# A decoder trunk on one core: the tile scheduler plans with its detailed timeline instead of a plain duration per instruction

## The chip, the cores and the metric

The kernel runs on one core of one Trainium2 chip. The time is device time in microseconds (us) of one execution, as the median of three runs of the kernel before: 2271.49 us (2265.71 to 2271.65). A core has five engines that each work through a list of instructions of their own, in order: PE (matmuls, with a weight load PEld for each), DVE (VectorE), ACT (ScalarE), POOL (GpSimd) and SP (SyncE, which here issues the DMAs). They wait for each other through semaphores.

## What is computed

Two residual layers and a final RMSNorm on an input of 1024 positions by 1024 channels, all float32. The even layer feeds dilated attention and a gated linear recurrence (HGRN2) from one projection; the odd layer is a gated DeltaNet with 16 value heads that share 8 key heads.

```python
def reference(x, norm_w, final_norm_w, even_w_in, even_w_out, hgrn_lb_logits, hgrn_norm_w,
              odd_w_in, odd_conv_w, odd_dt_bias, odd_a_log, odd_norm_w, odd_w_out):
    ...
    h = x
    for layer in range(DEPTH):
        hn = rms_norm(h, norm_w[layer])
        j = layer // 2
        if layer % 2 == 0:
            h = h + even_mixer(hn, even_w_in[j], even_w_out[j], lb_all[j], hgrn_norm_w[j])
        else:
            h = h + odd_mixer(hn, odd_w_in[j], odd_conv_w[j], odd_dt_bias[j], odd_a_log[j],
                              odd_norm_w[j], odd_w_out[j])
    return rms_norm(h, final_norm_w)
```

The part of the odd layer that matters here is the chunked delta rule. `sol` inverts a unit lower triangular matrix for each chunk, and `step` runs over the chunks in sequence, since each needs the state of the last:

```python
    lower = jnp.where(strict, jnp.einsum('bhnid,bhnjd->bhnij', kb, kc) * decay, 0.0)
    a_mat = lower + jnp.eye(C_CHUNK, dtype=jnp.float32)
    sol = lax.linalg.triangular_solve(a_mat, rhs, left_side=True, lower=True, unit_diagonal=True)
    ...
    def step(state, inp):
        u_n, w_n, a_n, qd_n, kt_n, gl_n = inp
        v_new = u_n - jnp.einsum('bhcd,bhdv->bhcv', w_n, state)
        o = jnp.einsum('bhcd,bhdv->bhcv', qd_n, state) + jnp.einsum('bhij,bhjv->bhiv', a_n, v_new)
        new_state = state * gl_n[..., None, None] + jnp.einsum('bhcd,bhcv->bhdv', kt_n, v_new)
        return new_state, o
```

## The kernel before

**Stages.** The kernel runs the norm and the transposes first (to about 57 us), then the HGRN2 heads of the even layer mixed with the projections of the next head (to about 460), the dilated attention with its output projection (to about 1060), the second norm and the odd layer's gates (to about 1210), the odd layer's eight heads (to about 2105), and its output projection with the final norm.

**Projections.** Every projection splits both operands into a high and a low part and accumulates three matmuls for each product (`mm3`, lines 151 to 153). In the rows of this document a matmul of these lines with the tile `pk`, `pv`, `pq` (the odd layer's key, value and query) or `oz` (its gate) is such a projection matmul of 128 by 512. They are called fill below: apart from their weights, they depend on nothing that the recurrence makes.

**A head of the odd layer** consists of four generators. `recur(hh)` (line 1149) goes through eight chunks of 128 positions. In chunk c, `vp` (L1197, PE) gives `vt` (L1200, DVE) and `vn` (L1202, ACT); `kv` (L1206, PE) takes `vt`, `op` (L1217, PE) takes `vn` and the attention tile `A` (L1170, DVE, from `qk`, L1168, PE); `kv` gives the new state `S` (L1210, DVE); the next chunk's `ks` (L1182, PE) and `qs` (L1188, PE) need `S`; `r` (L1185, DVE) comes from `ks`, `oq` (L1191, ACT) from `qs`, and the next `vp` needs `r`. `vp`, `qs` and `qk` share one PSUM bank (tag "d"), so that `vp` also has to wait until `oq` has read `qs`. `oj` (L1225, ACT) sums the squares of the output.

`invert(hh + 1)` (line 1044) prepares the triangular inverse of the next head. It has eight decay tables `gcl`, one for each chunk, which go through two buffers: a DMA (L1040), three activations on ACT (L1054 twice, L1055) and two operations on DVE (L1069), which scale `kk` (L1063, PE) into `L` and so set the buffer free. A 31-step substitution on DVE follows (L1084 and L1086), and then small matmuls. The recurrence has decay tables of its own (`gca`: DMA, POOL L1156, ACT L1158).

`proj(hh + 1)` (line 971) makes the next head's keys, values and queries, and first calls `way_out(hh - 1)` (line 1017) for the head before: `normed` (POOL L1005), the gate projection `oz` with its tile `g` (ACT L991, DVE L992, one buffer), the transposes `ot` (L1012, PE), `oy` (ACT L1013, POOL L1014) and a store to `ymix` (L1015).

**What sets the order.** The program is first written out in one sequence by generators that are mixed by weights:

```python
        for hh in range(8):
            fill = proj(hh + 1) if hh < 7 else seq(way_out(6), gate7(), out_last(range(3), ["pj"]))
            if hh < 7:
                fill = blend(invert(hh + 1), fill, 0.8)
            mix(recur(hh), fill, 2.8)
            drain(fill)
```

The tile scheduler of the context then sets each engine's order. It walks the program with that sequence as priority and, for each engine, issues in its planned time what is ready; the engines execute the resulting lists. Where `tc.manual_schedule` stands (PE in the attention, PE and DVE in its last part and the first output projection, lines 789 and 795) an engine keeps the order in which the program is written. Everything else on every engine goes by the planned time, which the scheduler before takes from a plain duration for each instruction. The context is opened in `kernel()`, below with the line numbers of the profile.

## Time and profile before

| | us |
|---|---|
| median of three runs | 2271.49 |
| lowest and highest | 2265.71, 2271.65 |
| the profiled execution | 2270.35 |
| its span, first to last instruction | 2268.6 |
| PE busy, share of the span | 2162.0, 95% |
| DVE busy | 1409.7, 62% |
| ACT busy | 950.0, 42% |
| POOL busy | 239.5, 11% |
| mean granted TensorE clock (1 is full speed) | 0.992 |

The profile's page gives the busy time of each engine, the span in 40 slices of equal length (a digit is the busy share in tenths; the row PEclk is the granted clock), and the costliest groups of instructions. The trace behind it answers by windows, by waits and by single rows in order of time. In a row of the timeline the first two numbers are the start and the duration in us; `[1.12 <-ACT oq L1191]` says that the engine sat idle for 1.12 us before it and that `oq` on ACT ended this.

### The profile page before, as it was taken

How to read it: one execution, taken by the hardware profiler on the slowest of the kernel's cores; microseconds unless marked ns; L12 is line 12 of the kernel's file. 1: busy time of each engine (PE TensorE's matmuls, PEld its weight loads, DVE VectorE, ACT ScalarE, POOL GpSimd, SP SyncE). 2: the span in 40 equal slices, each digit the busy share in tenths (PEclk: the TensorE clock that was granted, in tenths of full speed). 3: DMA queues.
4: the chain of work that ended last, by engine and by line, in shares of the span. 5: the costliest groups of instructions: out<-in, count | busy, mean ns of one | idle time of the engine just before them, and what ended most of it. 6: DMA issues, size and time to landing. Idle time of an engine off the chain costs nothing. (4 is left out here: it accounts for less than half of the span.)

```text
span 2268.6 us, 52553 instructions
## 1 busy us (share of the span) xinstructions
PE 2162.0 (95%) x21781; PEld 1760.6 (78%) x21781; DVE 1409.7 (62%) x3236; ACT 950.0 (42%) x2551; POOL 239.5 (11%) x252
## 2 busy tenths in 40 slices
PE   7999999999999999989999988989898999899998
PEld 6888888898877878767886776767777777678787
DVE  6353535453444344457776986968878787755767
ACT  5233333333232232222237664655555555544223
POOL 0010101010000000000000013121212121210000
PEclk9999999999999999989999999999999999999999
DMA  4111111114342334353233222121212122124233
GB/s 146 38 48 48 43 49 47 48 34 126 91 128 71 109 91 122 97 162 108 93 116 104 61 55 67 51 78 41 77 51 76 49 71 65 58 64 153 85 112 112
DMA packets 100079, 184.15 MB, mean 81 GB/s; under 512 B 12672, under 2 KB 30208, under 8 KB 99840
## 3 DMA queue, kind: packets, MB, share of 16 engines
q1 hardware_dynamic: 99840, 180.79, 25.9%
q8 instruction: 171, 2.80, 0.5%
q14 instruction: 68, 0.56, 0.1%
HBM read 151.25 MB, written 29.49 MB: 80 GB/s over the span
## 5 line engine op out<-in xcount | busy, mean ns | idle before, releaser
L117 DVE TENSOR_TENSOR w_lo<-raww,w_hi 128x512 fp32r<-128x512 f32 x292 | 210.2, 722 | 199.5 <-ACT w_hi L116 196.8
L116 ACT CAST w_hi<-raww 128x512 fp32r<-128x512 f32 x292 | 181.1, 620 | 298.0 <-DMA raww<-in_ewo_dram 51.0
L647 ACT ACTIVATE P<-P,nm 128x256 f32<-128x256 f32 (+7 forms) x128 | 71.4, 559 | 133.9 <-DVE nm L645 133.9
L151 PE MATMUL op<-w_hi,yplo 128*128 128x512 f32 x288 | 113.7, 395 | 3.3 <-DVE hr L296 1.7
L153 PE MATMUL op<-w_hi,yplo 128*128 128x512 f32 x288 | 112.2, 390 | 0.0
L152 PE MATMUL op<-w_lo,yplo 128*128 128x512 f32 x288 | 112.2, 390 | 0.0
L151 PE MATMUL oz<-hn_hi,w_hi 128*128 128x512 f32 x256 | 109.9, 429 | 0.0
L151 PE MATMUL pv<-hn_hi,w_hi 128*128 128x512 f32 x256 | 106.7, 417 | 0.5 <-ACT uv L899 0.5
L296 DVE TENSOR_TENSOR hr<-hr,op 128x512 f32<-128x512 f32 x128 | 85.9, 684 | 34.2 <-PE op L153 33.6
L153 PE MATMUL pv<-hn_hi,w_lo 128*128 128x512 f32 x256 | 104.1, 407 | 0.0
L152 PE MATMUL oz<-hn_lo,w_hi 128*128 128x512 f32 x256 | 103.0, 402 | 0.0
L153 PE MATMUL oz<-hn_hi,w_lo 128*128 128x512 f32 x256 | 102.5, 400 | 0.0
L152 PE MATMUL pv<-hn_lo,w_hi 128*128 128x512 f32 x256 | 102.2, 399 | 0.0
L653 DVE STREAM_TRANSPOSE PB<-P 128x256 f32<-128x256 f32 (+3 forms) x64 | 54.6, 853 | 72.8 <-ACT P L647 72.8
L1156 POOL TENSOR_TENSOR gca<-gca,MA 128x256 f32<-128x256 f32 x64 | 50.6, 791 | 453.8 <-DMA gca<-gcd 252.8
L296 DVE TENSOR_TENSOR hres<-hres,op 128x512 f32<-128x512 f32 x96 | 64.7, 682 | 31.8 <-PE op L153 29.4
L642 DVE CUSTOM_DVE_ANT_0 P<-S,G 128x256 f32<-128x256 f32 (+7 forms) x128 | 58.2, 492 | 36.8 <-PE S L638 35.2
L904 DVE SCALAR_TENSOR_TENSOR vT<-uv,cws,vT 128x512 f32<-128x512 f32 x96 | 74.3, 774 | 4.7 <-ACT vT L902 3.8
L1084 DVE TENSOR_TENSOR tm<-Lp,Tp 128x126 f32<-128x126 f32 (+22 forms) x248 | 74.9, 302 | 3.7
L1158 ACT ACTIVATE gca<-gca,g_ngc 128x128 f32<-128x128 f32 x128 | 45.8, 401 | 69.3 <-POOL gca L1156 69.1
L151 PE MATMUL avp<-w_hi,hn_hi 128*128 128x256 f32 x256 | 74.5, 291 | 0.0
L151 PE MATMUL op<-w_hi,yphi 128*128 128x512 f32 x160 | 65.9, 412 | 8.5 <-ACT yphi L116 4.6
(367 smaller groups left out, 6292.1 us busy)
## 6 DMA issues: line engine op xcount, KB each, us to landing
raww<-in_ew_dram SPq DMA_DIRECT2D x128, 256.0 KB, 3.0
raww<-in_ow_dram SPq DMA_DIRECT2D x100, 256.0 KB, 3.0
V<-vd SPq DMA_DIRECT2D x64, 256.0 KB, 5.3
rawy<-ymix SPq DMA_DIRECT2D x64, 256.0 KB, 2.7
raww<-in_ewo_dram SPq DMA_DIRECT2D x32, 256.0 KB, 3.0
gcl<-gcd SPq DMA_DIRECT2D x64, 128.0 KB, 3.0
gca<-gcd SPq DMA_DIRECT2D x64, 128.0 KB, 3.0
ymix<-oy SPq DMA_DIRECT2D x32, 256.0 KB, 2.0
```

The lines of the kernel that those rows point to most:

```text
L116: act.copy(hi, raw)
L117: dve.tensor_tensor(lo, raw, hi.bitcast(F32), op=ALU.subtract)
L151: pe.matmul(ps, lh, rh, start=start, stop=False)
L152: pe.matmul(ps, lh, rl, start=False, stop=False)
L153: pe.matmul(ps, ll, rh, start=False, stop=stop)
L296: dve.tensor_tensor(dst[:, n], src[:, n], ps, op=ALU.add)
L642: dve.tensor_tensor_reduce(Pm[:, e, w0:], S[e][:, w0:WG], G[:, w0:], 1.0, -3e38, op0=ALU.add, op1=ALU.max, accum_out=mx[:, e:e + 1])
L647: act.activation(Pm[:, e, w0:], Pm[:, e, w0:], AF.Exp, bias=nmx[:, e:e + 1], scale=0.125, accum_out=den[:, i, e:e + 1])
L653: dve.transpose(PB[:, :, i * WG + w0:(i + 1) * WG], Pm[:, :, w0:])
L904: dve.scalar_tensor_tensor(a[0][:, s], ub[:, i + s.start:i + s.stop], cws[:, tile_no, i:i + 1], a[0][:, s], op0=ALU.mult, op1=ALU.add)
L1084: dve.tensor_tensor(tm[:, :31 - k, :n], Lp[:, k, k + 1:, None].to_broadcast([P, 31 - k, n]), Tp[:, k:k + 1, :n].to_broadcast([P, 31 - k, n ...
L1156: pool.tensor_tensor(DA, DA, MA[:, None, :].to_broadcast([P, 2, 128]), op=ALU.add)
```

## The change

One argument of the tile context:

```diff
-    with tile.TileContext(nc) as tc:
+    with tile.TileContext(nc, schedule_with_timeline_sim=True) as tc:
         trunk_kernel(tc, *args)
```

The scheduler takes the planned time, which decides what is issued next on each engine, from its detailed timeline (a model of engines, semaphores and DMAs) instead of a plain duration for each instruction. No code of the kernel changes, and both kernels have the same instructions but for two loads of activation tables on ACT (26 before, 24 now). The order on all engines in the HGRN stage and in the odd layer is another; in the attention (some 500 to 1200 us) and from the last output projection on it stands as it was.

In the rows of order that follow, the digit after a tile's letters is the head, the next the chunk (`vp4_1` is `vp` of head 4, chunk 1), and the last number only tells tiles apart; "x2" stands for two instructions alike. `w46` and `w55` are weights, `hn` is the normed input, and `L4` holds head 4's inverse.

PE, before, from the end of head 3's recurrence into head 4's; the rows left out at "..." are projection matmuls of `oz` (11, 5 and 6 of them):

```order
L1168 MATMUL qk4_0_19968<-q4_19824,kT4_18183 128x128
L151 MATMUL oz3_0_0_19950<-hn_hi1_13909,w55_hi1_19639 128x512
...
L1012 MATMUL ot3_0_0_19988<-ident_69,bv3_18473 128x128 x4
L1197 MATMUL vp4_0_19996<-bv4_19691,L4_18651 128x128 x2
L151 MATMUL oz3_0_1_20003<-hn_hi0_13908,w55_hi0_19633 128x512
...
L1063 MATMUL kk5_1_20010<-kT5_19401 128x128 x4
...
L1206 MATMUL kv4_0_20044<-vt4_0_19999,kn4_18333 128x256
L1217 MATMUL op4_0_20048<-vn4_0_20001,A4_0_19970 128x128 x2
L1168 MATMUL qk4_1_20056<-q4_19824,kT4_18183 128x128
```

PE, of the change, at the same place, without a gap:

```order
L1197 MATMUL vp3_7_19780<-r3_7_19750,L3_17433 128x128 x2
L1063 MATMUL kk5_0_19876<-kT5_19401 128x128
L1217 MATMUL op3_7_19797<-vn3_7_19783,A3_7_19729 128x128 x2
L1168 MATMUL qk4_0_19968<-q4_19824,kT4_18183 128x128
L1197 MATMUL vp4_0_19996<-bv4_19691,L4_18651 128x128 x2
L1206 MATMUL kv4_0_20044<-vt4_0_19999,kn4_18333 128x256
L1217 MATMUL op4_0_20048<-vn4_0_20001,A4_0_19970 128x128 x2
L1168 MATMUL qk4_1_20056<-q4_19824,kT4_18183 128x128
L1182 MATMUL ks4_1_20089<-S4_0_20046,kT4_18183 128x256
L1063 MATMUL kk5_1_20010<-kT5_19401 128x128 x4
L1188 MATMUL qs4_1_20094<-S4_0_20046,q4_19824 128x256
L1197 MATMUL vp4_1_20112<-r4_1_20091,L4_18651 128x128 x2
```

No projection matmul stands between `vp` of chunk 7 and `vp` of chunk 2 of the next head; the fill that stood there now stands in the chunks before and after.

ACT, before, at `vn` of head 4's chunk 0 (`raww` is a weight being split):

```order
L1055 ACTIVATE gcl5_3_19895<-gcl5_3_19895 128x256
L1013 ACTIVATE oy3_0_0_19987<-ot3_0_0_19988,onws_14228 128x512
L1158 ACTIVATE gca4_2_20051<-gca4_2_20051,g_ngc_14219 128x128 x2
L1054 ACTIVATE gcl5_4_19902<-gcl5_4_19902,g_ngc_14219 128x128 x2
L1202 COPY vn4_0_20001<-vp4_0_19996 128x256
L1055 ACTIVATE gcl5_4_19902<-gcl5_4_19902 128x256
L1054 ACTIVATE gcl5_5_20015<-gcl5_5_20015,g_ngc_14219 128x128
L116 CAST w56_hi3_19944<-raww56_3_19946 128x512
```

ACT, of the change, from `vn` of head 3's last chunk to `vn` of head 4's chunk 0 and on:

```order
L1202 COPY vn3_7_19783<-vp3_7_19780 128x256
L1225 ACTIVATE oj3_7_0_19801,oss3_18645<-bv3_18473 128x128
L1225 ACTIVATE oj3_7_1_19803,oss3_18645<-bv3_18473 128x128
L1054 ACTIVATE gcl5_2_19888<-gcl5_2_19888,g_ngc_14219 128x128 x2
L1054 ACTIVATE gcl5_3_19895<-gcl5_3_19895,g_ngc_14219 128x128 x2
L1055 ACTIVATE gcl5_2_19888<-gcl5_2_19888 128x256
L1202 COPY vn4_0_20001<-vp4_0_19996 128x256
L1055 ACTIVATE gcl5_3_19895<-gcl5_3_19895 128x256
L1158 ACTIVATE gca4_2_20051<-gca4_2_20051,g_ngc_14219 128x128 x2
```

`vn` of chunk 0 came behind the activations of `gcl` 4; now it comes behind those of `gcl` 2 and 3, so that `gcl` 4 to 7 fall between the next chunks' `vn` and `oq`.

PE, before, in head 0 from `op` of chunk 3 to `vp` of chunk 4:

```order
L1217 MATMUL op0_3_15912<-vn0_3_15883,A0_3_15800 128x128 x2
L1168 MATMUL qk0_4_15920<-q0_15141,kT0_14333 128x128
L1182 MATMUL ks0_4_15935<-S0_3_15909,kT0_14333 128x256
L151 MATMUL oz0_0_0_16296<-hn_hi0_13908,w46_hi0_15818 128x512
L1188 MATMUL qs0_4_15940<-S0_3_15909,q0_15141 128x256
L152 MATMUL oz0_0_0_16296<-hn_lo0_13910,w46_hi0_15818 128x512
...
L1197 MATMUL vp0_4_15986<-r0_4_15937,L0_14534 128x128 x2
```

PE, of the change, in head 0 from `op` of chunk 3 to `op` of chunk 4, without a gap:

```order
L1217 MATMUL op0_3_15912<-vn0_3_15883,A0_3_15800 128x128 x2
L1168 MATMUL qk0_4_15920<-q0_15141,kT0_14333 128x128
L1182 MATMUL ks0_4_15935<-S0_3_15909,kT0_14333 128x256
L1188 MATMUL qs0_4_15940<-S0_3_15909,q0_15141 128x256
L1197 MATMUL vp0_4_15986<-r0_4_15937,L0_14534 128x128 x2
L1206 MATMUL kv0_4_16012<-vt0_4_15989,kn0_14523 128x256
L1217 MATMUL op0_4_16017<-vn0_4_15991,A0_4_15922 128x128 x2
```

In head 0 all eight chunks now stand on PE without a projection matmul; those that stood among them come ahead of its first `vp`.

## Prediction

> **What bounds the kernel now.** I read the page first, then the waits, then windows cut at the odd layer's heads, then the timeline inside them. The busy times, the 40 slices, and the longest waits of TensorE (engine, tile and line waited for, total us, times, longest):
>
> ```profile
> span 2268.6 us, 52553 instructions
> PE 2162.0 (95%) x21781; PEld 1760.6 (78%) x21781; DVE 1409.7 (62%) x3236; ACT 950.0 (42%) x2551; POOL 239.5 (11%) x252
> PE   7999999999999999989999988989898999899998
> DVE  6353535453444344457776986968878787755767
> ...
> PE op L1217 <- ACT vn L1202: 11.0, 14, 1.6
> PE nt L224 <- DVE xn L220: 10.5, 2, 8.3
> PE ks L1182 <- DVE S L1210: 9.7, 7, 1.8
> PE vp L1197 <- ACT oq L1191: 7.2, 10, 1.6
> ```
>
> PE bounds the kernel. Its amount of work does not change here, so the time is that work plus what PE loses in waits, and only the second part can move. Three of the four waits shown belong to `recur`, the delta-rule recurrence of the odd layer (`nt` is in the norms), and VectorE is close behind PE there (7 to 9 tenths). So I cut the odd layer where `vt` of chunk 0 starts in each head (columns: us, busy time of each engine, PEclk, DMA share, GB/s):
>
> ```profile
> 1319.00:1401.00 82.00, 71.26 (x543) 55.95 (x543) 63.59 (x177) 43.65 (x128) 20.06 (x24) 0.94 0.22 61
> 1401.00:1491.50 90.50, 84.73 (x619) 67.03 (x618) 74.94 (x219) 55.35 (x174) 18.69 (x21) 0.98 0.19 54
> 1491.50:1599.40 107.90, 98.21 (x697) 79.51 (x695) 85.25 (x232) 61.21 (x185) 20.84 (x23) 1.00 0.22 65
> 1599.40:1707.60 108.20, 99.93 (x698) 80.84 (x698) 85.51 (x226) 60.87 (x182) 20.88 (x23) 1.00 0.22 62
> 1707.60:1814.60 107.00, 99.72 (x698) 80.84 (x698) 85.11 (x226) 60.83 (x183) 22.12 (x25) 1.00 0.21 62
> ```
>
> "Busy" overstates PE, since pipelined matmuls overlap. The rhythm at which they follow each other is what one costs:
>
> ```profile
> 1505.43 0.60 PE L1206 MATMUL kv<-vt,kn 128*128 128x256 f32 x2
> 1505.87 0.61 PE L1217 MATMUL op<-vn,A 128*128 128x128 f32 x4
> 1506.31 0.39 PE L1168 MATMUL qk<-q,kT 128*128 128x128 f32 x2
> 1506.45 0.48 PE L151 MATMUL oz<-hn_hi,w_hi 128*128 128x512 f32 x1
> ...
> 1508.85 0.39 PE L152 MATMUL oz<-hn_lo,w_hi 128*128 128x512 f32 x1
> 1509.08 0.39 PE L153 MATMUL oz<-hn_hi,w_lo 128*128 128x512 f32 x1
> 1509.31 0.59 PE L1182 MATMUL ks<-S,kT 128*128 128x256 f32 x2
> ```
>
> A projection matmul costs 0.23 us (1508.85 to 1509.08), `kv` and `op` 0.44 each, `qk` 0.14. With `ks` and `qs` at about 0.43 and `vp` near 0.3 a chunk of the recurrence costs PE 2.0 us. A full head is 288 projection matmuls (66.3 us), eight chunks (16) and about 9 for inversion and transposes: 91 us of work in a window of some 108. **PE loses about 17 us per full head**, and by the same count 25 us in head 0 and 18 in head 1. Of some 155 us lost in eight heads, much could be gained or added to.
>
> **The change part by part.** No instruction of weight is added or removed (two activation-table loads on ACT go). The planner's order moves. The order of attention (500 to 1200 us) and of the tail stands as before: nothing to count. The HGRN stage and the odd layer are re-ordered.
>
> *Heads 3 to 5.* In the order before, the projection matmuls ahead of each `vp` of a head come 36, 30, 20, 22, 36, 42, 36 and 66 per chunk: spread. Afterwards 0, 0, 69, 66, 55, 55, 43 and 0. Thus from `vp` of chunk 7 to `vp` of chunk 2 of the next head PE has no fill: only 8.7 us of its own work (three chunks, `kk`, `ot`). This stretch also holds six of the eight rounds in which `invert` of the next head makes its decay tables (`gcl`, two buffers) and scales `kk`:
>
> ```profile
> 1403.21 1.13 DVE L1069 SCALAR_TENSOR_TENSOR L<-kk,sc,gcl 128x128 f32<-128x128 f32 x4 [0.49 <-PE kk L1063]
> ...
> 1420.55 0.60 DVE L1069 SCALAR_TENSOR_TENSOR L<-kk,sc,gcl 128x128 f32<-128x128 f32 x2
> ...
> L1054 ACT ACTIVATE gcl<-gcl,g_ngc x128: 384/392/433, 1235.7 to 1932.3; 128x128 f32<-128x128 f32 x128
> L1069 DVE SCALAR_TENSOR_TENSOR L<-kk,sc,gcl x128: 336/343/352, 1238.2 to 1933.9; 128x128 f32<-128x128 f32 x128
> L1040 SPq DMA_DIRECT2D gcl<-gcd x64: 319/320/1868, 1231.9 to 1928.2; - x64
> L1055 ACT ACTIVATE gcl<-gcl x64: 399/410/423, 1237.8 to 1933.2; 128x256 f32<-128x256 f32 x64
> ...
> DMA to landing us min/median/max: 2.8/3.0/5.2
> ```
>
> One buffer's round is a DMA of 3.0, ACT 2 x 0.39 + 0.41 and DVE 2 x 0.34: 4.9 us. After the first two, three rounds follow in each buffer: 14.7, with the first pair's 0.7 about 15.4 at least. The trace took 1403.2 to 1421.1, 17.9 us, in head 2's. ACT now holds `vn` and `oq`, for which PE's `op` and `vp` wait, in order behind `gcl` activations that wait for that DMA. So I set the stretch by the ring at 17.6 (nearest row 17.9, floor 15.4), plus a lead of 0.9 and some 3.3 until `vp` of chunk 2, whose ACT queue still holds `gca` (2 x 0.4), `oy`, `oj` and `g`: 21.8 us, 13 of them idle. SP and POOL do not relieve it: on SP the same `gcl` loads stand in the same sequence, only the `ymix` stores now come behind them; on POOL the multiplication at L1005 moves behind one more `gca`. The other 82 us of PE work then have 43 to 69 projection matmuls (10 to 16 us) per chunk beside the chain from one `vp` to the next:
>
> ```profile
> 1501.25 0.49 PE L1197 MATMUL vp<-r,L 128*128 128x128 f32 x2 [1.12 <-ACT oq L1191]
> ...
> 1502.89 0.42 DVE L1200 TENSOR_TENSOR vt<-vp,g_etl 128x256 f32<-128x256 f32 x1 [1.57 <-PE vp L1197]
> ...
> 1507.57 0.60 DVE L1210 SCALAR_TENSOR_TENSOR S<-S,g_egl,kv 128x128 f32<-128x128 f32 x2
> ...
> 1512.05 0.60 DVE L1185 SCALAR_TENSOR_TENSOR r<-ks,sc,bv 128x128 f32<-128x128 f32 x2
> ...
> L1084 DVE TENSOR_TENSOR tm<-Lp,Tp 128x126 f32<-128x126 f32 (+22 forms) x31 | 9.3, 301 | 0.7
> L1086 DVE TENSOR_TENSOR Tp<-Tp,tm 128x126 f32<-128x126 f32 (+22 forms) x31 | 8.8, 284 | 0.6
> ```
>
> [...] Ten and more us of fill cover that, so the short waits there vanish. What is late next is VectorE: of its 85 us per head some 64 fall to four covered chunks, 16 on average and up to 18.7 where most of the inversion's substitution (L1084 and L1086, 18 us per head) stands, against PE's 17 to 18. I leave 5 us of loss for that (bounds 2 and 12). A head becomes 13 + 5 = 18 against 16.7 lost now: +1.4, three times **+4**.
>
> *Head 0* gets no projection matmul in any of its eight chunks; about 118 of them (27.5 us) run ahead of its first `vp` instead. PE's work from its `vt0` to head 1's falls from 57 us to 25. Of VectorE's 64 us in that window 45 stay (18 of them that substitution), and a bare chain of 8 chunks costs 8 x 4.5 = 36, some 39 with its start. If they overlap fully it takes 45, if not at all 84; I take the middle, 64, so 39 idle against 25 now: **+14** (from -5 to +34). The work pulled ahead fills waits in front of it: -2. *Head 1* has 62 to 67 matmuls in each of four chunks, then four nearly bare chunks (22 us for 14 of work, 8 idle): 13 lost against 18, **-5**. *Head 2* likewise **-6**. Head 6 about 0, head 7 +1. Odd layer without the clock: 4 + 14 - 2 - 5 - 6 + 1 = **+6**.
>
> *The clock.* After stretches in which PE was busy only in part, the granted clock halves:
>
> ```profile
> 1372.00:1379.00 7.00, 3.15 (x15) 1.78 (x13) 6.86 (x25) 1.38 (x3) 4.30 (x5) 1.00 0.07 19
> 1379.00:1389.30 10.30, 8.18 (x83) 6.45 (x83) 7.48 (x14) 3.04 (x5) 7.32 (x10) 0.50 0.24 78
> ...
> 1474.50:1478.00 3.50, 2.25 (x103) 1.75 (x102) 3.44 (x7) 0.89 (x2) 0.74 (x2) 1.00 0.00 0
> 1478.00:1481.40 3.40, 3.40 (x10) 2.64 (x10) 3.31 (x7) 1.55 (x3) 0.00 (x0) 0.50 0.35 107
> ```
>
> A window at 45% busy and one at 64% were each followed by 0.50. The bare stretches are 40% busy (8.7 of 21.8; 25 of 64). I expect about seven of them, each leaving at least one half-clock window of 3.4 us under full load, a loss of 1.7: 12. Head 0's chain runs partly at half clock: its 2 us of PE per chunk would grow by up to 8 in all, I take 5. Before has 17 us of such windows in these heads, 8.6 lost, which go or stay: 12 + 5 - 9 = **+8** (bounds 0 and 16). [...]
>
> *HGRN stage.* Its window:
>
> ```profile
> 60.00:460.00 400.00, 398.27 (x5079) 338.35 (x5079) 182.35 (x338) 142.86 (x362) 37.57 (x36) 1.00 0.14 46
> ```
>
> PE has no more than 1.7 us idle in 400 (27 us by the rhythm, nearly all within the fill), and VectorE and ACT are under half busy. Spread otherwise, the chain stays covered but for a few places: **+1.5** (from -10 to +10).
>
> Sum: 2270.35 of the profiled execution + 6 + 8 + 1.5 = 2285.9. That execution lies 1.1 below the median of the runs (2271.49), and 1.75 beyond its span, which stays. Carried to the median: **2287 us**.
>
> **The rivals.** *Faster*: the dense chunks shed all their waits (s = 2 instead of 5 in six heads, -18), the ring runs near its floor (-2 in five stretches, -10), and no clock falls (-8); head 0 as forecast. 2287 - 36 = 2251. For it: 155 us of loss are there to be taken, and PE's waits in heads 2 to 7 are short and many, as fill removes them. Against: the ring's rows, of which none is at the floor. It decides where stretch loss plus s goes under 16.7 per head, that is at a ring under about 16. *No measurable change* (within 0.3%, 6.8 us, about what a measurement of this kernel can tell): s = 3 in six heads (-12) and a clock term of +3 (-5): 2270. *Much slower*: VectorE becomes the bound in the covered chunks. Its in-order queue then has to hold 18.7 us where PE has 17.9, with hand-offs on top, s = 12 in six heads: +42, 2329. For it: DVE is 79% busy in a full head already, and 45 us of its work in head 0 stand where PE has little. That the flag does nothing is excluded where the order moved, and holds for attention and tail.
>
> **How the numbers follow.** Forecast (2278 to 2312) 0.45, much slower 0.15, no change 0.2, faster 0.2. The range reaches from the faster case to the much slower one, 2252 to 2330, and leaves out about 0.2 beyond both. Slower by over 0.3%: 0.45 + 0.15 = 0.6; within: 0.2; faster: 0.2.
>
> **What would show it.** In the profile of the changed kernel: `vt` of head 0 near 1343 and of head 1 near 1407; five stretches per head change of about 22 us at 40% PE; `op` waiting for `vn` and `vp` for `oq` there, ACT's `gcl` waiting for its DMA; PEclk below 1 behind them; covered chunks of 17 to 19 us with hardly a wait of PE. Wrong if heads 3 to 5 are under 105 us apart (the ring is shorter than I take it), if the clock holds at 1.00, or if PE waits for VectorE in covered chunks (the heavy rival).

## Result and profile after

The changed kernel takes **2364.05 us** (median of four runs, 2362.89 to 2365.72), the kernel before 2270.68 beside it (2265.71 to 2271.65): a ratio of **1.0416, 95% interval 1.0398 to 1.0434**. The sign was as forecast, the size was not: +93 us against +16, and outside the range of 2252 to 2330. The profiled execution took 2363.97 us with a span of 2361.8 and a mean granted clock of 0.961 (0.992 before). One execution of a later kernel, `tl_la1`, took 11615 us for a reason that is not known, and its ratio leaves that execution out.

The page after, the lines that answer to those shown of before (busy times, and the clock in 40 slices):

```profile
span 2361.8 us, 52491 instructions
...
PE 2223.3 (94%) x21781; PEld 1815.0 (77%) x21781; DVE 1400.1 (59%) x3236; ACT 943.7 (40%) x2549; POOL 229.9 (10%) x252
...
PEclk9999999999999999999999976979998999999999
```

The same 21781 matmuls keep PE "busy" 61 us longer. That is no more work: at a granted clock of 0.50 `op` lasts 1.22 us (in the rows below), at 1.00 it lasts 0.61 (in the row of before). The other 32 of the 93 us are idle time of PE (138.5 us of the span, 106.6 before). The clock falls to 0.7, 0.6 and 0.7 in the 24th, 25th and 27th slice (1358 to 1476 and 1535 to 1594 us), which are head 0 and the change from head 1 to head 2. TensorE's longest waits after (total us, times, longest):

```profile
PE vp L1197 <- ACT oq L1191: 21.4, 18, 3.9
PE op L1217 <- ACT vn L1202: 19.7, 13, 3.3
```

They were 7.2 and 11.0 before. The odd layer cut at `vt` of chunk 0, after: heads 0, 1, 2 and 4 (us, busy times, PEclk, DMA share, GB/s):

```profile
1375.80:1458.80 83.00, 61.00 (x397) 44.56 (x398) 48.54 (x153) 35.34 (x112) 17.58 (x22) 0.57 0.15 40
1458.80:1565.00 106.20, 100.51 (x672) 82.13 (x671) 79.85 (x220) 55.48 (x174) 11.49 (x16) 0.94 0.19 54
1565.00:1677.70 112.70, 102.92 (x698) 84.96 (x698) 81.76 (x222) 60.34 (x182) 20.44 (x23) 0.95 0.22 60
1789.90:1902.90 113.00, 104.36 (x698) 86.37 (x698) 83.65 (x225) 60.25 (x182) 20.05 (x23) 0.94 0.20 59
```

Beside the windows of before, the 93 us come about as follows. Projection matmuls move between the windows, so the last two columns give how many more of them (L151 to L153) start in a window after than before, and the difference without them, at 0.23 us each.

| | before | after | difference | projection matmuls more | difference without them |
|---|---|---|---|---|---|
| `vt` of chunk 0, head 0, at | 1319.3 | 1375.8 | +56.5 | +116 | +29.8 |
| head 0 | 81.8 | 83.0 | +1.2 | -135 | +32.3 |
| head 1 | 90.4 | 106.2 | +15.8 | +51 | +4.1 |
| head 2 | 107.9 | 112.7 | +4.8 | +10 | +2.5 |
| heads 3, 4, 5 | 108.2, 107.0, 108.1 | 112.2, 113.0, 112.1 | +4.0, +6.0, +4.0 | 0 | +14.0 |
| head 6 | 99.3 | 102.0 | +2.7 | -1 | +2.9 |
| head 7 and what follows | 246.6 | 244.8 | -1.8 | -41 | +7.6 |

The first row holds some 27 us of projection matmuls that were pulled ahead of head 0. They are not lost in themselves, but head 0, with 19 projection matmuls in place of 154, did not become any shorter for it. Cut once more, head 0 of after reads (from `vt` of chunk 0 to that of chunk 2; the next four bare chunks; the end of the recurrence and the inversion; the rest):

```profile
1375.80:1396.90 21.10, 12.43 (x48) 10.07 (x48) 9.08 (x29) 10.22 (x37) 1.45 (x2) 0.66 0.24 54
1396.90:1427.70 30.80, 23.59 (x65) 14.86 (x64) 22.91 (x77) 12.71 (x45) 2.37 (x4) 0.50 0.09 23
1427.70:1445.00 17.30, 11.96 (x184) 8.93 (x184) 12.31 (x40) 5.98 (x21) 7.88 (x12) 0.50 0.12 32
1445.00:1458.80 13.80, 13.02 (x101) 10.70 (x102) 4.24 (x7) 6.43 (x12) 5.88 (x6) 0.67 0.18 63
```

For 48 us the clock stays at 0.50, although PE is at work for 24 of 31 us in the second row. One of these chunks in the timeline of after:

```profile
1412.31 1.23 PE L1197 MATMUL vp<-r,L 128*128 128x128 f32 x4 [0.78 <-ACT oq L1191]
...
1414.06 1.22 PE L1206 MATMUL kv<-vt,kn 128*128 128x256 f32 x2 [0.52 <-DVE vt L1200]
...
1415.18 1.22 PE L1217 MATMUL op<-vn,A 128*128 128x128 f32 x4
...
1416.20 0.63 PE L1168 MATMUL qk<-q,kT 128*128 128x128 f32 x2
1416.62 1.06 PE L1182 MATMUL ks<-S,kT 128*128 128x256 f32 x2
...
1417.48 1.16 PE L1188 MATMUL qs<-S,q 128*128 128x256 f32 x2
...
1418.74 0.62 ACT L1191 ACTIVATE oq<-qs,g_eg 128x128 f32<-128x128 f32 x2 [1.07 <-PE qs L1188]
1419.41 1.23 PE L1197 MATMUL vp<-r,L 128*128 128x128 f32 x4 [0.77 <-ACT oq L1191]
```

From `vp` to `vp` 7.1 us pass. `op` to `qk` takes 1.02 us here and took 0.44 at full clock (1505.87 to 1506.31 us in before). Nothing fills PE, so its own six steps in a row are most of the chain, and the last link is not `r` but `oq`: `vp` shares its PSUM bank with `qs` and has to wait until ACT has read it. Head 7's start has bare chunks too, at full clock, of 5.3 and 4.8 us:

```profile
2117.00:2122.30 5.30, 3.35 (x18) 2.33 (x18) 3.74 (x16) 2.15 (x9) 1.99 (x3) 1.00 0.20 41
2122.30:2127.10 4.80, 4.45 (x28) 3.33 (x27) 2.33 (x7) 3.03 (x11) 4.68 (x5) 1.00 0.09 25
```

The first three intervals between the `vt` of head 0 are longer still, 10.3, 10.8 and 9.5 us, and for another reason:

```profile
1382.15 0.69 ACT L1054 ACTIVATE gcl<-gcl,g_ngc 128x128 f32<-128x128 f32 x2 [5.50 <-DMA gcl<-gcd]
...
1384.22 0.60 ACT L1191 ACTIVATE oq<-qs,g_eg 128x128 f32<-128x128 f32 x2
...
1384.87 1.23 PE L1197 MATMUL vp<-r,L 128*128 128x128 f32 x4 [3.88 <-ACT oq L1191]
```

ACT has `oq` in its list behind `gcl` activations, which wait 5.50 us for their DMA, and PE stands 3.88 us. The ring of the decay tables thus lies in head 0 as well as at the changes of heads.

At the change of heads, the place of the other forecast, the rows from head 3 to head 4 are these:

```profile
1791.41 0.69 ACT L1054 ACTIVATE gcl<-gcl,g_ngc 128x128 f32<-128x128 f32 x2 [1.94 <-DMA gcl<-gcd]
...
1793.18 0.40 ACT L1055 ACTIVATE gcl<-gcl 128x256 f32<-128x256 f32 x1
1793.48 0.35 ACT L1202 COPY vn<-vp 128x256 f32<-128x256 f32 x1
1793.88 1.22 PE L1217 MATMUL op<-vn,A 128*128 128x128 f32 x4 [2.83 <-ACT vn L1202]
...
1809.61 1.22 PE L1197 MATMUL vp<-r,L 128*128 128x128 f32 x4 [0.91 <-ACT oq L1191]
```

ACT waits for the DMA of a `gcl`, `vn` stands behind it, and `op` waits 2.83 us for `vn`.

### The profile page after: what moved, and what is told of

It reads as the page before. It is cut to its first block, busy times and chain, and to the rows that moved or that the text cites. A ratio compares the mean times of both kernels' runs of the same rounds, so it can differ in the third digit from the quotient of the medians.

```text
span 2361.8 us, 52491 instructions
## 1 busy us (share of the span) xinstructions
PE 2223.3 (94%) x21781; PEld 1815.0 (77%) x21781; DVE 1400.1 (59%) x3236; ACT 943.7 (40%) x2549; POOL 229.9 (10%) x252
## 5 line engine op out<-in xcount | busy, mean ns | idle before, releaser
L117 DVE TENSOR_TENSOR w_lo<-raww,w_hi 128x512 fp32r<-128x512 f32 x292 | 205.1, 704 | 226.0 <-ACT w_hi L116 216.9
L151 PE MATMUL op<-w_hi,yplo 128*128 128x512 f32 x288 | 113.9, 397 | 3.9 <-DVE hres L296 1.7
L153 PE MATMUL op<-w_hi,yplo 128*128 128x512 f32 x288 | 111.6, 390 | 0.0
L151 PE MATMUL oz<-hn_hi,w_hi 128*128 128x512 f32 x256 | 105.1, 410 | 0.0
L151 PE MATMUL pv<-hn_hi,w_hi 128*128 128x512 f32 x256 | 103.6, 405 | 1.2 <-ACT uv L899 1.2
L153 PE MATMUL oz<-hn_hi,w_lo 128*128 128x512 f32 x256 | 102.9, 402 | 0.0
L153 PE MATMUL pv<-hn_hi,w_lo 128*128 128x512 f32 x256 | 102.7, 401 | 0.0
L152 PE MATMUL pv<-hn_lo,w_hi 128*128 128x512 f32 x256 | 102.0, 398 | 0.0
L296 DVE TENSOR_TENSOR hres<-hres,op 128x512 f32<-128x512 f32 x96 | 64.5, 681 | 29.8 <-PE op L153 29.1
L1069 DVE SCALAR_TENSOR_TENSOR L<-kk,sc,gcl 128x128 f32<-128x128 f32 x128 | 37.2, 344 | 63.0 <-ACT gcl L1055 47.7
L151 PE MATMUL avp<-w_hi,hn_hi 128*128 128x256 f32 x256 | 74.1, 289 | 0.0
L151 PE MATMUL bip<-w_hi,hn_hi 128*128 128x256 f32 x256 | 73.3, 286 | 0.0
```

Of the source, the lines that this page charges most:

```text
L117: dve.tensor_tensor(lo, raw, hi.bitcast(F32), op=ALU.subtract)
L151: pe.matmul(ps, lh, rh, start=start, stop=False)
L152: pe.matmul(ps, lh, rl, start=False, stop=False)
L153: pe.matmul(ps, ll, rh, start=False, stop=stop)
L296: dve.tensor_tensor(dst[:, n], src[:, n], ps, op=ALU.add)
```

## The experiments

A planner answers every edit with another order. The most telling kernels are therefore those that do not let it: the order of one kernel is written down as a table and laid on the other as issue-order edges (an instruction may not be issued on its engine before its predecessor in the table; no semaphore is added). The lines of these kernels come 17 to 21 later than in the profile of before; L1218 and L1214 are its L1197.

```diff
+def pin(tc, nc):
...
+        row = [ins[k + d] for k, d in enumerate(place)]
+        for u, v in zip(row, row[1:]):
+            tc.add_manual_dep(v, u.name, mybir.DependencyInfo(mybir.DependencyClass.NoSync, mybir.DependencyReason.DATA), reason="order")
...
+    pin(tc, nc)
```

Ratios are to the kernel before, run on the same chip in the same group.

### Which stages carry the 93 us

Three kernels with the planner of before have on all engines the order of after in one part only: `p_even` up to the odd layer, `p_h0` in the odd layer's start and head 0, `p_h1` from head 1 on.

> The kernel before, with all engines held to the changed kernel's order up to the first instruction of the odd layer's program (start, HGRN stage, attention, first output projection, second norm); the odd layer is planned as before. By the trace of the changed kernel, which was 17 us late at the output projection's end and lost some 7 more in the norm behind it: 2286 to 2298. If the plain planner makes up for it in the odd layer, or those losses are shifted work: under 2280.

> The kernel before, with all engines held to the changed kernel's order in the odd layer's start and head 0 (up to the first instruction of head 1's recurrence in the program). By the trace (6 us more idle time ahead of head 0, 33 in it): 2300 to 2315, with a granted clock of about 0.57 to 0.7 in head 0. If a bare head 0 costs no more than the held-back fill of the run with head 0 bare under the plain planner (27): 2290 to 2300.

> The kernel before, with all engines held to the changed kernel's order from the first instruction of head 1's recurrence to the end. If the parts add up (93 less 25 for the even stages and 39 for the start with head 0): 29 us, 2292 to 2306, heads 3 to 5 at 110 to 113 us. If the parts hang together: under 2285 or over 2315.

| | median us | ratio | 95% interval | over before |
|---|---|---|---|---|
| p_even | 2294.51 | 1.0108 | 1.0086 to 1.0131 | +24.7 |
| p_h0 | 2308.48 | 1.0171 | 1.0140 to 1.0201 | +38.7 |
| p_h1 | 2310.72 | 1.0187 | 1.0170 to 1.0204 | +42.4 |

The first two came as expected, the third 5 us above its bounds, with heads 3 to 5 at 112.0, 112.4 and 114.7. The parts add up to 105.8 against 93.4, a surplus hardly larger than their intervals allow. It does not lie behind head 1: from the first `vt` of head 1 to the end, `p_h1` takes 903.9 us and after 903.0 (867.5 before). What `p_h1` has more is in head 0, which takes 85.5 us there, a window that `p_h0` reaches into as well. Each part slows the kernel, and the one ahead of the odd layer, for which the prediction had 1.5 us, is a quarter of the whole. In `p_h0`, head 0 reads

```profile
1352.20:1437.30 85.10, 59.26 (x406) 41.82 (x406) 48.52 (x154) 34.88 (x112) 17.57 (x22) 0.66 0.15 41
```

with a mean clock of 0.66: the order alone makes the bare head, and with it the low clock.

For `p_even`, the waits of TensorE up to head 0 in before and then in `p_even` (same columns as above):

```profile
PE nt L224 <- DVE hn_lo L227: 2.8, 3, 1.6
```

```profile
PE nt L245 <- DVE hn_lo L248: 6.3, 5, 2.3
PE o L688 <- issue: 3.3, 1, 3.3
PE S L654 <- DVE mx L663: 3.1, 1, 3.1
```

and what after's clock does behind two such holes (2.4 us between the transposes `nt` at 38.2 us, then 0.50 from 41.1 to 44.5; 3.1 us in front of the attention's `S` at 553.8, then 0.50 from 556.6 to 563.2):

```profile
40.00:65.00 25.00, 24.25 (x145) 21.68 (x146) 9.95 (x18) 6.83 (x16) 0.00 (x0) 0.93 0.14 43
...
555.00:575.00 20.00, 18.07 (x252) 13.67 (x256) 7.43 (x25) 6.03 (x18) 1.26 (x1) 0.83 0.73 191
```

That the orders ahead of the odd layer cost 25 us is measured. Where they arise is read from the traces alone: `p_even` is 4.0 us behind before at the first `bip` (a projection of the HGRN stage; 49.8 and 53.8 us), 13.2 at the first `o` of the attention (553.1 and 566.3), 15.2 at its last (1056.3 and 1071.5) and 21.6 at the last `nt` of the second norm (1204.1 and 1225.7). So some 4 us are lost at the start, 9 up to the seam between HGRN and attention, 2 in the attention with its output projection and 6 in the second norm. In the norm VectorE's order is not that of before, other than said above of everything from 500 to 1200 us: between the last six `xn` (L220) it has six splits of odd-layer weights (`w_lo`, L117), where it had three. How much of this is the holes themselves and how much the half clock behind them is not told apart.

### What the half clock is worth in head 0

The next three kernels keep the plan's mode of after and add matmuls whose result is never read, three per bare chunk behind `qs`: `tl_warm0` in head 0, in the unused half of `qs`'s bank; `tl_warmb` in head 0 in a bank of its own; `tl_warmall` in such a bank in all chunks of head 0 and in chunks 1 and 2 of the other heads. A written matmul of this size is two records in the trace (three more in a chunk take its records from 16 in after to 22).

```diff
-                    qs = bank("d", [P, 2, 128], f"qs{hh}_{c}")
-                    pe.matmul(qs, q[:, s], St, start=True, stop=True)
+                    qs = bank("d", [P, 4, 128], f"qs{hh}_{c}") if hh == 0 else bank("d", [P, 2, 128], f"qs{hh}_{c}")
+                    pe.matmul(qs[:, 0:2, :], q[:, s], St, start=True, stop=True)
+                    for _ in range(3 if hh == 0 else 0):
+                        pe.matmul(qs[:, 2:4, :], kT[:, s], St, start=True, stop=True)
```

> The changed kernel with three more matmuls per chunk of head 0, of the size of ks, behind qs, which write to an unused half of the bank of qs and are read by nobody: PE's order in head 0 stays without fill. Theory (the clock that is halved sets the length of head 0): the added matmuls keep PE busy, the granted clock in head 0 rises from 0.57 to over 0.85, and its eight chunks go from 83 us to 62 to 72 although PE has more to do. Rival (the chain's waits set it, the clock is only a consequence): clock up or not, head 0 takes 83 to 95.

> The changed kernel with the three added matmuls per chunk of head 0 in a bank of their own and behind qs, so that oq no longer waits for them (in the first form it did, at some 1.3 us per chunk, and a bare chunk took 6.3 to 6.6 us at full clock instead of 7.1 at half). If the halved clock costs 2 us per bare chunk, a bare chunk now takes 5.0 to 5.8 us at a granted clock of 1.0 and head 0 70 to 74 us; if the clock costs less than 1 us per chunk, 6.2 or more and over 76.

> The changed kernel with three more matmuls behind qs, in a bank of their own and read by nobody, in all chunks of head 0 and in chunks 1 and 2 of every other head, where it is bare. If the halved clock carries some 2 us per bare chunk and 2 us behind each bare stretch, the granted clock rises from 0.961 to over 0.98 and the time falls by 15 to 30 us, to 2334 to 2349. If the clock is worth little, it stays at 2354 to 2364.

`tl_warm0`: 2357.07 us, ratio 1.0381 (1.0365 to 1.0396). Head 0 and one of its chunks:

```profile
1376.10:1452.90 76.80, 55.46 (x439) 42.99 (x440) 49.74 (x154) 34.95 (x112) 17.83 (x22) 0.84 0.16 43
1411.60:1417.90 6.30, 4.81 (x22) 3.30 (x22) 5.65 (x22) 2.18 (x9) 0.57 (x1) 1.00 0.07 21
```

With more work on PE the clock is 1.00 in the three chunks in the middle (0.50 in after), and they are shorter (6.3 to 6.6 us for 7.1) although `oq` now waits for the added matmuls as well. So the half clock is a cause of the slow chunks, and the edit leaves what stands ahead where it was (`vt` of head 0 at 1376.1, 1375.8 in after). Head 0 gains 6 us of the 83, less than expected (62 to 72). The three chunks at full clock save 2 us in all, since the added matmuls now stand in their chain. The first three intervals hardly change (10.1, 10.3 and 8.5 us, though the clock is 0.80 to 0.83 in them): `vp` waits 8.1 us for `oq` there, behind the `gcl` ring. `tl_warmb`, 2359.15 us, 1.0395 (1.0377 to 1.0413), has one chunk of 5.3 us at full clock, but others of 6.4; its head 0 takes 88.0, with 21 projection matmuls more at its end (some 5 us), so it measures another plan. `tl_warmall`, 2384.65, 1.0504 (1.0486 to 1.0521), was expected to be the fastest of them and is 20 us slower than after. Why is not shown: `kv` waits 15.6 us for `vt` in all, 8.5 in after, and every head is planned anew.

The same question from the other side: `pl_bare0` is the kernel before with the fill of head 0 taken out of its chunks (32 steps of it drained ahead, and an issue-order rule that keeps it there).

> The kernel before, plain planner, with the fill of head 0 written ahead of its recurrence (168 projection matmuls go ahead of its first vp) and the rule that no projection passes the last vp in that head: head 0 has no projection matmul in any chunk, as in the changed kernel; all other engines and all other heads stay with the plain plan. Theory (a bare head 0 and the clock that halves in it cost the 33 us by themselves): granted clock of 0.5 to 0.65 in head 0, bare chunks of about 7 us, the time 2290 to 2310. Rival (the other engines' orders of the timeline are needed for that loss): within 12 us of 2271.

2297.98 us, 1.0122 (1.0103 to 1.0141). A chunk of head 0:

```profile
1357.40:1364.20 6.80, 4.79 (x16) 3.10 (x16) 5.12 (x19) 2.28 (x9) 0.72 (x1) 0.75 0.06 19
```

Under the plain planner a bare chunk is about as slow, 6.8 us at a mean clock of 0.75, and head 0 takes 78.1. Its first three intervals, though, are 7.7, 6.9 and 6.8 us where after has 10.3, 10.8 and 9.5, which points to the order of the other engines for those. But `pl_la1` below, with the same kind of rule for all heads and fill left in head 0, has `vt` of head 2 at the same time (1521 to 1522, 30 later than before). What bareness costs beyond the rule is therefore not told apart: inconclusive for the sum, clear for the chunk.

### Is it the fill that PE pulls ahead?

My theory after the result was that PE's fill, pulled ahead and bunched, is the whole cause, and that spreading it again under the detailed timeline would give most of the loss back. The rule: a projection's first matmul may be issued only behind the last `vp` that precedes it in the program. `tl_la1` has it with the planner of after, `pl_la1` with that of before, `tl_laall` as `tl_la1` and in the HGRN stage too.

```diff
-        pe.matmul(ps, lh, rh, start=start, stop=False)
+        i = pe.matmul(ps, lh, rh, start=start, stop=False)
+        if start and len(VP) >= 1:
+            tc.add_manual_dep(i.ins, VP[-1].name, mybir.DependencyInfo(mybir.DependencyClass.NoSync, mybir.DependencyReason.DATA), reason="fill")
```

> The changed kernel with one rule more: in the heads of the odd layer no projection may start on PE ahead of the last vp that the program has written before it (an issue order on PE alone, no wait on a semaphore). The detailed timeline then spreads the projection matmuls 48, 24, 24, 24, 24, 48, 48, 48 per chunk, much like the kernel before, and head 0 gets them too; all other engines are still ordered by the timeline. Theory 1 (fill pulled ahead on PE, bare chunks behind it, the clock halved in them): heads 0 to 6 lose about what they lost before, the time falls from 2364 to 2290 to 2315. Rival (the orders of ACT and VectorE carry it, as the two kernels with PE by hand suggest, which stand 106 us apart with the same order on PE): the time stays at 2340 to 2400, and PE waits for oq and vn.

> The kernel before with the same rule. Its planner already spreads the projection matmuls as the program does (36, 30, 21, 21, 36, 42, 36, 66 with the rule); control: 2260 to 2285 by both theories. What stands between this and the timeline with the rule is the other engines' order and the stages ahead of the heads: 15 to 40 by theory 1, over 70 by the rival.

> As the run before with the timeline and the rule, with the rule in the HGRN stage too (no projection ahead of the last group of the chain's matmuls that the program has written before it). If fill pulled ahead in that stage made the 14 us that the changed kernel has lost by the time the attention runs, most of it comes back: 8 to 12 us under the timeline with the rule in the heads alone. If it was the first norm or the other engines' order: within 4 us of it.

| | median us | ratio | 95% interval |
|---|---|---|---|
| tl_la1 | 2396.58 | 1.0552 | 1.0533 to 1.0571 |
| pl_la1 | 2297.32 | 1.0116 | 1.0098 to 1.0134 |
| tl_laall | 2437.53 | 1.0734 | 1.0717 to 1.0752 |

**The theory fell.** In `tl_la1` every chunk has its fill again (24 or 48 projection matmuls), and the kernel is 32 us slower than after, with heads 0 to 5 at 110 to 118 us. The rule by itself costs 27 (`pl_la1`, expected at 2260 to 2285: head 1's fill may no longer start in head 0); the other 99 between the two kernels come from what the planner does with the same rule and include the stages ahead. `tl_laall`, expected at or below `tl_la1`, lies 41 us above it, and its head 0 starts 42 us later (`vt` at 1387.2 and 1345.4), so the rule costs that much ahead of the heads. The longest wait of TensorE in `tl_la1`, and two rows of its ACT:

```profile
PE vp L1201 <- ACT oq L1195: 27.8, 22, 4.5
```

```profile
1862.07 0.63 ACT L911 ACTIVATE uk<-kT 128x512 f32<-128x512 f32 x1 [4.26 <-DVE kT L908]
1862.61 0.35 ACT L1207 COPY vn<-vp 128x256 f32<-128x256 f32 x1
```

`vp` waits longer for `oq` than it did in after, though PE has fill: ACT's list holds an activation of the next head's keys ahead of `vn`, and idles 4.26 us for it. `op` waits less for `vn` (3.6 us in all, 19.7 in after), but `ks` waits 19.3 us for `S` (3.6 in after). The lists of ACT and DVE, which wait for each other, thus hold PE up in `tl_la1` (27.8 us at `vp`, 19.3 at `ks`) with fill in every chunk.

PE in the order in which the program is written, under both planners (`tl_pehand`, `pl_pehand`), and the same in the HGRN stage alone on after (`tl_pehg`):

```diff
-            mix(recur(hh), fill, 2.8)
-            drain(fill)
+            with tc.manual_schedule(engines={mybir.EngineType.PE}):
+                mix(recur(hh), fill, 2.8)
+                drain(fill)
```

> The changed kernel, but PE keeps the program's own order in the eight heads of the odd layer (36, 30, 18, 24, 36, 42, 36, 66 projection matmuls ahead of each vp instead of 0, 0, 69, 66, 55, 55, 43, 0; head 0 gets fill too). All other engines are still ordered by the detailed timeline. Theory (the loss is PE's order: chunks without fill, and the halved clock in them): head 0 falls from 83 us to 70 or less of its own loss, the heads 3 to 5 from 112 to about 107, and the time from 2364 to 2295 to 2310, since what was lost ahead of the heads (some 25 us) stays. Rival (the order of ACT behind gcl and of VectorE carries it): op goes on waiting for vn and vp for oq, and the time stays over 2340.

> The kernel before with the same PE order by the program in the heads. Control: its PE order is close to that of before (36, 30, 20, 22, ...), so both theories expect 2255 to 2290. The difference to the run with the timeline and the same PE order is what the other engines' order and the stages ahead of the heads cost: about 25 by the theory, over 60 by the rival.

> The changed kernel with PE in the program's own order in the HGRN stage. The +14 us that the changed kernel has gathered by the time the attention runs should fall to under 4 if PE's order in that stage made it (bt to S0_1 waited 3.3 us there, then the clock halved): about 2352. If the first norm (nt, +4) or the order of the other engines made it, it stays at 8 to 14: 2358 to 2366. The odd layer's order is planned anew and may differ by some us.

They took 2524.47 (1.1115, 1.1098 to 1.1132), 2418.48 (1.0648, 1.0630 to 1.0666) and 2380.48 (1.0481, 1.0462 to 1.0500): the first lies where its rival had it (over 2340), the other two above everything expected. A written order blocks PE in the inversion, in `tl_pehand` (and in `pl_pehand`, with 158.2 us):

```profile
PE qp L1107 <- DVE Un L1090: 137.1, 8, 25.6
```

With PE's list in the heads the same in both, the planner of after is still 106 us slower than that of before, of which some 25 belong to the stages ahead: its orders of the other engines cost something apart from PE's.

Last, the bunching alone: `pl_bareb` is the kernel before with the fill of heads 2 to 6 held in chunks 2 to 5 (72 projection matmuls each, fewer in head 6, none in the others).

> The kernel before, plain planner, with the fill of heads 2 to 6 written and held in chunks 2 to 5 (72 matmuls each, 24 short in head 6), so that four chunks at each of five changes of head are bare on PE (three in the changed kernel). Theory (a bare change of head costs 13 us of idle time and saves most of the short waits elsewhere, with the clock halved behind it): heads 3 to 6 grow by 4 to 9 us each over before, 2290 to 2315. Rival (bare chunks are harmless under the plain order of ACT and VectorE): within 10 us of 2271.

2347.39 us, 1.0331 (1.0315 to 1.0347). Heads 2 to 6 take 117.6 to 122.8 us, 13 to 18 more each, where I had expected 4 to 9 for heads 3 to 6. Some of that is the inversion in a new place (`qp` waits 28.1 us for `Un` in all), so it bounds the price of bunching from above and does not measure it.

### Which engine's order

If no rule on the fill helps, one engine's list might. Four kernels with laid orders in the odd layer: before's planner with PE in after's order (`p_oddpe`) or with ACT and DVE in it (`p_oddad`); after's planner with PE in before's order (`t_oddpe`) or with ACT and DVE in it (`t_oddad`). The engines not named are planned anew.

> The kernel before, with PE held to the changed kernel's order in the odd layer, the other engines planned plainly around it. If PE's bare chunks carry the odd layer's loss: 2325 to 2350, heads 3 to 5 at 110 to 114 us. If the orders are worth something only as a set: 2360 or more. If PE's order does no harm without the others: under 2300.

> The kernel before, with ACT and VectorE held to the changed kernel's order in the odd layer, PE, POOL and SP planned plainly around them. If these orders carry the loss: 2325 to 2350. If only the set counts: 2360 or more. If they do no harm without PE's order: under 2300.

> The changed kernel, with PE held to the order of the kernel before in the whole odd layer; the other engines are planned by the detailed timeline around it. If PE's order carries the loss of the odd layer (some 65 us): 2285 to 2310. If the timeline's orders of ACT and VectorE do: 2335 or more.

> The changed kernel, with ACT and VectorE held to their order of before in the odd layer, PE, POOL and SP planned by the timeline around them. If PE's order carries the loss: 2345 to 2370. If the orders of ACT and VectorE do: 2285 to 2315.

| | median us | ratio | 95% interval |
|---|---|---|---|
| p_oddpe | 2355.85 | 1.0382 | 1.0367 to 1.0398 |
| p_oddad | 2405.01 | 1.0603 | 1.0584 to 1.0621 |
| t_oddpe | 2391.96 | 1.0542 | 1.0521 to 1.0563 |
| t_oddad | 2462.61 | 1.0855 | 1.0834 to 1.0876 |

PE's new list is enough to lose 87 us with everything else planned plainly (`p_oddpe`, between its two ranges), about as much as all engines' new orders in the same place (38.7 and 42.4). Head 0 there:

```profile
1348.90:1432.80 83.90, 58.49 (x397) 43.65 (x398) 46.89 (x155) 35.42 (x112) 17.78 (x22) 0.62 0.15 40
```

But PE's old list cures nothing (`t_oddpe`, 28 us slower than after). Every mixture of two plans is slower than before by 87 to 193 us, and three of the four are slower than after itself. The waits of `t_oddpe` point to why:

```profile
PE qp L1124 <- DVE Un L1107: 39.7, 7, 8.2
PE op L1234 <- ACT vn L1219: 27.3, 22, 3.0
PE vp L1214 <- ACT oq L1208: 24.6, 9, 5.3
```

PE, in before's order, comes to the inversion and to `op` when the newly planned DVE and ACT have not been there yet. The lists of five engines are one plan: none of the lists taken out of it here was of use beside the others.

## Why the prediction was right in sign and wrong in size

**Right.** PE's work does not change, and the time is what PE loses in waits and clock. The place at the change of heads is as described: `vp` of chunk 7 in head 3 to `vp` of chunk 2 in head 4 took 23.2 us (1786.4 to 1809.6; forecast 21.8), with `op` waiting for `vn` behind the `gcl` activations and these for their DMA. The two bare and two covered chunks behind `vt` of head 4 follow. The covered ones take 20.7 and 18.6 us (17 to 19 forecast), with VectorE nearly as busy as PE; but no wait of PE is listed in the four covered chunks (1810.9 to 1885.2 us), so that the heavy rival is out:

```profile
1789.90:1801.40 11.50, 6.91 (x28) 5.37 (x28) 5.63 (x23) 6.17 (x22) 4.51 (x5) 0.70 0.26 60
1801.40:1810.90 9.50, 6.71 (x29) 5.86 (x30) 4.24 (x14) 6.88 (x21) 3.93 (x5) 0.73 0.30 87
1810.90:1831.60 20.70, 20.70 (x98) 17.28 (x98) 19.34 (x49) 13.70 (x46) 4.17 (x4) 0.96 0.25 75
1831.60:1850.20 18.60, 18.60 (x93) 15.61 (x92) 17.65 (x55) 10.56 (x37) 0.73 (x1) 1.00 0.20 65
```

The clock falls in the bare stretches (0.70 and 0.73 above); the longest single wait of PE between 1785 and 1811 us is the 2.83 us of `op`.

**Head 0, +14 - 2 and +5 of the clock.** Measured by `p_h0`: 38.7 for 17. The picture was right as far as it went (a bare head, and some 27 us of its fill ahead of it), but 64 us was forecast for its window and 83 came. That 83 lies next to the 84 of no overlap at all is chance, since VectorE's substitution does run under the bare chunks (VectorE is busy for 22.91 of 30.80 us in the second row of head 0). The step that failed is the price of a bare chunk, 4.5 us by the state's path (`vp`, `vt`, `kv`, `S`, `ks`, `r`): 3.3 us of rows and 1.2 for six hand-offs between engines. No run shows the 1.2. Where the later engine stood idle, a hand-off from `vp` on to `r` took 0.03 to 0.06 us in before, and 0.14 to 0.15 from `S` to `ks`; from `oq`'s end at 1419.36 to `vp` at 1419.41 in after it is 0.05. At full clock the 4.5 holds fairly all the same (5.3 and 4.8 in head 7), although the path that closes there runs through PE's own sequence and the shared bank to `oq`. In head 0 it does not hold, for two reasons. The first three intervals took 30.6 us in place of 13.5, with ACT's `oq` behind the `gcl` ring: the sum had that ring at the changes of heads and left it out here. And the half clock was priced at 5 us for eight chunks, as if it came and went; it stayed at 0.50 for 48 us, and the next four chunks took 28.6 us in place of 18. Against some 5 us at full clock the half clock is thus worth about 2 us for each bare chunk, an estimate that `tl_warm0` supports in direction alone.

**Stages ahead of the odd layer, +1.5.** Measured by `p_even`: 24.7. I asked only whether the HGRN stage stays filled, and it does. The planner also moved the start, the seam between HGRN and attention, and the second norm, the last two in the part in which the prediction had nothing to count; there it left holes, and behind those of the start and the seam the clock was 0.50 for 3.4 and 6.6 us in after. This term was the largest miss beside its own size, and its range (-10 to +10) did not hold it. The attention itself stayed, as forecast (388.71 us busy of 390 in both traces).

**Heads 1 and 2, -11.** Head 1 came out 15.8 longer, of which some 12 are work (51 projection matmuls more); the rest, about +4, stands against the -5. For head 2 it is about +3 instead of -6. The failing step is the end of head 1: its four bare chunks were given 22 us and took 29.1 with a mean clock of 0.77, while the four covered chunks ahead of them ran at 1.00:

```profile
1458.80:1535.90 77.10, 75.15 (x372) 62.35 (x372) 62.18 (x173) 44.48 (x135) 5.26 (x6) 1.00 0.22 62
1535.90:1565.00 29.10, 25.36 (x302) 19.78 (x300) 17.67 (x48) 11.00 (x39) 6.23 (x10) 0.77 0.12 34
```

**Heads 3 to 5, +4, and the clock behind their stretches.** +14 together. With three of the seven stretches at 1.7 us of clock, 9 was forecast for them. The stretch was 1.4 us longer than taken in head 3's change. PE's idle time grew by 0.6, 1.4 and 0.7 us per head over before, its busy time with the same matmuls by 3.4, 4.6 and 3.3, at a mean clock of 0.94 to 0.95 in place of 1.00: the right mechanism, and the term that was too small is the clock's.

**Head 7, +1.** Without the 41 projection matmuls that stand ahead now, head 7 and what follows are some 8 us longer; where these lie was not followed up.

**The faster rival and "no change"** needed a ring at its floor and a clock that holds; neither came. The last doubt, what comes first, stays open: whether ACT's, DVE's or PE's list begins the loss in a given head cannot be told from mixtures that are all slower. A third `gcl` buffer, which would loosen the ring at the change of heads, was not tried. None of the versions run beats the kernel before.

## What to carry to other kernels

Judge a planner's new order by stages and as a whole: lay it on the old kernel stage by stage, since one or two engines' lists, taken from one plan into another, gave a kernel slower than before every time here. In the new order look first for stretches without fill on the engine that bounds, seams between stages included, and price them at the clock that such a stretch shows (here 0.50, and 7.1 us instead of some 5 per chunk), for as long as it lasts. Follow the chain in such a stretch through the engine's own sequence, through shared PSUM banks and through the lists of the engines that empty them, not only through the data: in head 0, `oq` stood behind activations that waited for a DMA.

## What the hardware showed unexpectedly

The granted clock stayed at 0.50 for 48 us, with PE busy about 5.8 of 7.1 us (at half speed) in each of the bare chunks in the middle of it, and a similar chunk with three matmuls more, busy 4.81 of 6.3, was granted 1.00:

```profile
1413.60:1420.70 7.10, 5.81 (x16) 3.72 (x16) 5.17 (x18) 2.27 (x9) 0.78 (x2) 0.50 0.06 18
```

The chunk that keeps the half clock looks busier than the one that has the full clock, so a busy share here says little without the clock at which it was reached. In `pl_bare0`, whose chunks have the same 16 matmul records in 6.8 us, the mean of 0.75 is an alternation:

```profile
1359.05:1362.47 3.42, 3.15 (x10) 2.28 (x10) 2.10 (x10) 0.92 (x5) 0.00 (x0) 0.50 0.00 0
1362.47:1365.88 3.41, 1.64 (x7) 0.82 (x6) 3.02 (x10) 1.52 (x7) 0.72 (x1) 1.00 0.13 38
```

A stretch at half clock that was busy 3.15 of 3.42 us was followed by full clock, and one at full clock that was busy 1.64 of 3.41, idle for 1.77 us in all, by half clock again (the next chunk's mean, 1364.2 to 1371.1 us, is 0.75 as well). What makes the clock turn was not measured.
